# First loads on one queue, first norm and first gate projection interleaved, sums of squares by token

## The chip, the cores and the metric

The kernel runs on one core of one Trainium2 chip, in one launch. The metric is device microseconds of one execution. Three executions of the kernel before took 999.3, 1000.33 and 1001.49 us, median 1000.33. The profile comes from one further execution.

## The reference

An encoder trunk of two layers over 256 tokens of width 1024, all in float32. Each layer is FFN, mixer, FFN, and every part is a residual branch behind an RMS norm. What matters here is the first norm and the first FFN:

```python
def rms_norm(x, g):
    y = x * rsqrt(mean(x * x, axis=-1) + EPS)
    return y * g

def swiglu_ffn(h, w_gu, w_down):            # w_gu: 1024 x 5632, w_down: 2816 x 1024
    gate, up = split(h @ w_gu, 2, axis=-1)
    return (silu(gate) * up) @ w_down

x = x + 0.5 * swiglu_ffn(rms_norm(x, norm_g[0, 0]), ffn_w_gu[0, 0], ffn_w_down[0, 0])
```

Then follow a chunked gated linear attention, two more FFNs, a differential softmax attention with a relative-position bias, and a last FFN. All weights, 177 MB in all, are read once.

## The kernel before, in words

**Precision.** Each float32 operand is split in two parts that TensorE multiplies at its faster rate: a high part (ScalarE copies it, rounded) and a low part (VectorE subtracts the high part from the original). A product is three partial products. `mm3` (L207) forms them with two instructions: the weight's high part against the high and low halves of the activations (512 columns, L210), and the weight's low part against the high half (256 columns, L211). One such couple of instructions is called a pair below.

**Weights.** `weight_plan` lists all weight blocks in the order of use, mostly 1024 x 256 (1 MB). `prefetch` (L137) issues their loads on SyncE's DMA queue (SP) into three `stage` buffers; the first two blocks are loaded in four parts of 256 KB. `parts` (L152) gives the operations that split a block, one couple (high on ScalarE, low on VectorE) for each part; `split_weights` (L171) issues them up to three blocks ahead of use. `next_weights` (L194) does both and hands out the block.

**The start.** L269 loads `cst` (identity, a triangle and a column of 1/1024; 128.5 KB) on ScalarE's queue. L275 loads the norm weights as `rows`, 48 x 128, on GpSimd's queue. TensorE multiplies zeros (`ps_idle`, L280), eight products in 16 recorded instructions. `first_norm` (L446) loads x by token into `x_tm` (256, 256 and 512 columns, L452) on SP and then calls `prefetch(0)`. TensorE transposes `rows` (L455; ScalarE copies the result to `par`) and all sixteen 128 x 128 blocks of x (L462) into four PSUM tiles. Then, in an order written out with `issue_after` (which ties an instruction to one before it on the same engine), ScalarE and VectorE alternate: two column blocks of x are split with the norm's weight as scale (L321, L322), then one part of the first weights (L471). After these VectorE copies x out of PSUM (`keep`, L475), the second weights are split (L481), and x is squared block by block on ScalarE (L330, L333) and added up on VectorE (L334).

**The first FFN.** `ffn` (L490) has eleven steps c; each projects a gate block and an up block of 256 columns with `project` (L213), 16 pairs each, into two PSUM banks. Only the first gate projection runs with `together=True`: block by block of x as it becomes ready. The norm's factor by token is not needed before the products are joined: `stats` (L336) multiplies the added squares by the column of 1/1024 on TensorE (`ps_ms`, L339, four recorded instructions), and VectorE forms the reciprocal root in eleven small instructions (`rsqrt`, L253). `spread` (L344) copies it over the partitions. `join` (L246) adds the halves of a projection and so frees its banks. At c = 3 `load_params` and `relative_bias` (L773) come; the latter loads a table and 64 KB of buckets on ScalarE's queue (L776, L778).

The order of instructions on an engine is planned by the compiler: it takes the first in program order that its own model holds to be ready, and ties keep their order. So an instruction can stand ahead of another that is written before it. PSUM has six banks under tag A and two under tag B.

Of the kernel before, what the change touches and what calls it, by code (L numbers as in the profile page):

```python
# [11 lines left out]
F32 = mybir.dt.float32  # L12
FR = mybir.dt.float32r
I32 = mybir.dt.int32
AF = mybir.ActivationFunctionType
ALU = mybir.AluOpType
AX = mybir.AxisListType

P = 128
# [97 lines left out]
def trunk(ctx: ExitStack, tc: tile.TileContext, ins, out):  # L117
# [76 lines left out]
    def next_weights():  # L194
        n = state["use"]
        state["use"] += 1
        prefetch(n)
        split_weights(n)
        return split.pop(n)
# [13 lines left out]
    def project(w, act, name, together=False):  # L213
        banks = [psA.tile([P, 512], F32, tag="A", name=f"{name}_{b}") for b in range(2)]
        order = [(b, k) for b in range(2) for k in range(KD)]
        for b, k in sorted(order, key=lambda bk: bk[1]) if together else order:
            mm3(banks[b], w, slice(b * P, (b + 1) * P), act, k, k == 0, k == KD - 1)
        return banks
# [50 lines left out]
    nc.scalar.dma_start(cst, ins["c_mats"])  # L269
# [5 lines left out]
    nc.gpsimd.dma_start(rows, ins["norm_g"].rearrange("l s (k p) -> (l s k) p", p=P))  # L275
# [37 lines left out]
    class Norm:  # L313
# [22 lines left out]
        def stats(self):  # L336
            ps = psB.tile([P, 512], F32, tag="B", name=f"ps_ms{self.idx}")
            for t in range(2):
                mm(ps[:, t : t + 1], lhsT=self.acc[:, t * P : (t + 1) * P], rhs=inv_d, start=True, stop=True)  # L339
            self.var = small.tile([P, 2], F32, tag="var", name=f"var{self.idx}")  # L340
            nc.vector.tensor_scalar(out=self.var, in0=ps[:, 0:2], scalar1=EPS, scalar2=None, op0=ALU.add)
            self.r = rsqrt(self.var, [P, 2], f"r{self.idx}")
# [103 lines left out]
    def first_norm():  # L446
        n = Norm(0)
        with ExitStack() as xctx:
            xp = xctx.enter_context(tc.tile_pool(name="xin", bufs=1))
            x_tm = xp.tile([P, 2, D], F32, name="x_tm")  # L450
            for cs in (slice(0, CW), slice(CW, D // 2), slice(D // 2, D)):
                nc.sync.dma_start(x_tm[:, :, cs], ins["x"][0].rearrange("(t p) c -> p t c", p=P)[:, :, cs])  # L452
            prefetch(0)
            pst = psB.tile([P, 512], F32, tag="B", name="ps_rows")
            nc.tensor.transpose(out=pst[:, 0:NG], in_=rows, identity=ident[0:NG, 0:NG])  # L455
            nc.scalar.copy(par, pst[:, 0:NG])

            tiles = [psA.tile([P, 2, T], F32, tag="A", name=f"ps_x{i}") for i in range(KD // 2)]
            xt = [tiles[k // 4 * 2 + k % 2][:, k // 2 % 2, :] for k in range(KD)]
            for k in range(KD):  # L460
                for t in range(2):
                    nc.tensor.transpose(out=xt[k][:, t * P : (t + 1) * P], in_=x_tm[:, t, k * P : (k + 1) * P], identity=ident)  # L462
            last = ()
            for kp, ops in enumerate(parts()):
                for k in (2 * kp, 2 * kp + 1):
                    with ExitStack() as order:
                        for i in last:
                            order.enter_context(tc.issue_after(i.ins))
                        last = n.split(k, xt[k])
                with tc.issue_after(last[0].ins), tc.issue_after(last[1].ins):  # L470
                    last = [op() for op in ops]  # L471

            def keep(kp):
                k = kp // 2 * 4 + kp % 2
                return nc.vector.tensor_copy(x[:, k : k + 3 : 2, :], tiles[kp])  # L475

            with tc.issue_after(last[1].ins):
                behind = [keep(0), keep(1)]
            with tc.issue_after(behind[1].ins), tc.issue_after(last[0].ins):
                for ops in parts():  # L480
                    last = [op() for op in ops]  # L481
            with tc.issue_after(last[1].ins):
                behind = [last[0], keep(2), keep(3)]
            state["behind"] = behind
            with tc.issue_after(last[0].ins), tc.issue_after(behind[2].ins):
                for k in range(KD):
                    n.square(k)
        return n

    def ffn(norm, nxt, first=False, beside=None):  # L490
        with ExitStack() as fctx:
            fp = fctx.enter_context(tc.tile_pool(name="ffn", bufs=2))
            a2 = fp.tile([P, NFB, 2, T], FR, tag="a2", name="a2", bufs=1)
            for c in range(FF // CW):
                if first and c == 3:
                    load_params()
                    relative_bias()
# [4 lines left out]
                pg = project(next_weights(), norm.x2, f"ps_g{c}", together=first and c == 0)  # L502
                if c == 0:
                    norm.stats()
                    if not first:
                        release(*state["behind"])
# [471 lines left out]
    norm = first_norm()  # L978
    with tc.tile_pool(name="gatew", bufs=1) as gw:
        w2 = gw.tile([P, 2, GH * DK], FR, name="w2")  # L980
        norm = ffn(norm, 1, first=True, beside=lambda: load_gate(w2))
        norm = gla(norm, 2, w2)
# [47 lines left out]
```

## Time and profile before

| what | us |
|---|---|
| median of three runs | 1000.33 |
| lowest, highest | 999.3, 1001.49 |
| the profiled execution, whole | 1001.98 |
| its span, first to last instruction | 1000.2 |
| TensorE busy in the span | 990.1 |
| VectorE, ScalarE busy | 747.1, 566.4 |
| DMA: bytes read, mean rate | 176.84 MB, 179 GB/s |

The span starts with the first recorded instruction; 1.8 us of the execution lie around it. Times of a row count from the span's start. "Busy" of TensorE (PE) counts a matmul from its start to a modelled end, so that a matmul whose predecessors are slow can look longer than it is; the distance from one start to the next is the better measure. PEld is TensorE's loading of the stationary operand. DVE is VectorE, ACT ScalarE, SP the SyncE queue, and a name with q is an engine's sequencer, where DMAs are issued.

### The profile page before, as it was taken

Reading aid. Unit: us, or ns where it says so; the run is one execution under the profiler, and the core shown is the slowest. Engines: PE = TensorE matmul, PEld = TensorE weight load, DVE = VectorE, ACT = ScalarE, POOL = GpSimd, SP = SyncE. Lnnn points to the kernel's source line nnn. Section 1 sums busy time; section 2 is a strip of 40 time slices with the busy share of each in tenths; the row PEclk is TensorE's granted clock in tenths of the full one; section 3 lists DMA queues with packets and bytes.
Section 4 is the critical chain, followed back from the end, with each engine's and each line's share of the span. In section 5 each row is a group of like instructions: output and inputs, shape, how many; then the busy total and the mean of one; then the engine's idle time right before and its main releaser. Section 6 shows DMA issues by size and latency. Waiting matters only on the chain.

```text
span 1000.2 us, 14797 instructions
## 1 busy us (share of the span) xinstructions
PE 990.1 (99%) x5834; PEld 869.7 (87%) x5834; DVE 747.1 (75%) x1282; ACT 566.4 (57%) x950; POOL 2.0 (0%) x10
## 2 busy tenths in 40 slices
PE   8999999999999999999999999999999999999998
PEld 7888888998889888888888888888778998888886
DVE  6998757499977987775679777656989689767540
ACT  6766535397746755543456655435586577555430
POOL 0000000000000000000000000000000000000000
PEclk9999999999999999999999999999999999999999
DMA  9686554665322875555557655375553268555430
GB/s 291 225 262 210 183 165 131 198 223 182 102 85 86 277 227 192 177 169 178 179 175 238 206 174 186 120 238 177 203 173 127 65 193 278 182 169 198 159 126 22
DMA packets 166339, 178.87 MB, mean 179 GB/s; under 512 B 4547, under 2 KB 154846, under 8 KB 166270
## 3 DMA queue, kind: packets, MB, share of 16 engines
q1 hardware_dynamic: 165982, 177.68, 54.9%
q8 instruction: 46, 0.75, 0.3%
q10 hardware_dynamic: 256, 0.21, 0.1%
q14 instruction: 23, 0.19, 0.1%
q0 software_dynamic: 32, 0.02, 0.0%
HBM read 176.84 MB, written 1.06 MB: 178 GB/s over the span
## 4 chain that ended last, share of the span: by engine, by line
PE 69%; DVE 5%; ACT 1%; DMA 1%; issue 0%; SPq 0%; ACTq 0%
PE ps_u L210 12%; PE ps_g L210 12%; PE ps_d L210 8%; PE ps_g L211 6%; PE ps_u L211 6%; PE ps_d L211 4%; PE ps_d L225 2%; PE ps_d L227 2%; PE ps_d L226 2%; DVE w L186 1%; PE ps_s L618 1%; PE ps_w L203 1%; PE ps_w L204 1%; PE ps_w L205 1%; PE ps_g L227 1%; PE ps_g L225 1%
## 5 line engine op out<-in xcount | busy, mean ns | idle before, releaser
L186 DVE TENSOR_TENSOR w<-stage,w 128x1024 fp32r<-128x1024 f32 x332 | 384.2, 1195 | 33.2 <-ACT w L186 33.1
L186 ACT ACTIVATE w<-stage 128x1024 fp32r<-128x1024 f32 x332 | 326.9, 1035 | 55.5 <-PE ps_d L227 15.3
L210 PE MATMUL ps_g<-x,w 128*128 128x512 f32 x704 | 249.5, 397 | 0.0
L210 PE MATMUL ps_u<-x,w 128*128 128x512 f32 x704 | 248.7, 395 | 0.0
L211 PE MATMUL ps_u<-x,w 128*128 128x256 f32 x704 | 197.3, 281 | 0.0
L211 PE MATMUL ps_g<-x,w 128*128 128x256 f32 x704 | 197.1, 281 | 0.0
L210 PE MATMUL ps_d<-a,w 128*128 128x512 f32 x528 | 183.2, 390 | 0.0
L210 PEld LDWEIGHTS ps_g<-x,w 128*128 128x128 f32 x704 | 132.1, 188 | 31.1 <-issue 0.9
L210 PEld LDWEIGHTS ps_u<-x,w 128*128 128x128 f32 x704 | 132.0, 188 | 30.8
L211 PE MATMUL ps_d<-a,w 128*128 128x256 f32 x528 | 148.9, 282 | 0.0
L211 PEld LDWEIGHTS ps_g<-x,w 128*128 128x128 f32 x704 | 133.4, 189 | 0.5
L211 PEld LDWEIGHTS ps_u<-x,w 128*128 128x128 f32 x704 | 133.0, 189 | 0.1
L210 PEld LDWEIGHTS ps_d<-a,w 128*128 128x128 f32 x528 | 99.1, 188 | 20.8
L211 PEld LDWEIGHTS ps_d<-a,w 128*128 128x128 f32 x528 | 99.8, 189 | 0.0
L321 ACT ACTIVATE x<-x,par 128x256 fp32r<-128x256 f32 x40 | 20.0, 507 | 117.8 <-DVE x L370 117.8
L250 ACT COPY half<-ps_u 128x256 f32<-128x256 f32 x88 | 32.7, 372 | 86.3 <-PE ps_u L211 84.6
L250 ACT COPY half<-ps_g 128x256 f32<-128x256 f32 x88 | 32.3, 370 | 80.0 <-PE ps_g L211 78.4
L251 DVE TENSOR_TENSOR gate<-ps_g,half 128x256 f32<-128x256 f32 x88 | 36.6, 419 | 38.0 <-ACT half L250 37.9
L251 DVE TENSOR_TENSOR up<-ps_u,half 128x256 f32<-128x256 f32 x88 | 36.6, 419 | 37.8 <-ACT half L250 37.8
L370 DVE SCALAR_TENSOR_TENSOR x<-ps_d,x 128x256 f32<-128x256 f32 x48 | 20.3, 423 | 57.9 <-PE ps_d L211 56.7
L225 PE MATMUL ps_d<-w,a 128*128 128x512 f32 (+1 forms) x90 | 35.2, 391 | 0.5 <-DVE xt L441 0.5
L226 PE MATMUL ps_d<-w,a 128*128 128x512 f32 (+1 forms) x90 | 35.1, 390 | 0.0
(239 smaller groups left out, 1335.9 us busy)
## 6 DMA issues: line engine op xcount, KB each, us to landing
stage<-in_ffn_w_gu_dram SPq DMA_DIRECT2D x86, 1024.0 KB, 5.3
stage<-in_ffn_w_down_dram SPq DMA_DIRECT2D x34, 1024.0 KB, 5.3
stage<-in_gla_w_in_dram SPq DMA_DIRECT2D x12, 1024.0 KB, 5.7
stage<-in_ffn_w_down_dram SPq DMA_DIRECT2D x12, 768.0 KB, 4.5
stage<-in_diff_w_in_dram SPq DMA_DIRECT2D x16, 512.0 KB, 5.6
stage<-in_gla_w_out_dram SPq DMA_DIRECT2D x4, 1024.0 KB
stage<-in_diff_w_in_dram SPq DMA_DIRECT2D x4, 1024.0 KB
stage<-in_diff_w_out_dram SPq DMA_DIRECT2D x4, 1024.0 KB
```

What stands on the lines that cost most here:

```text
L186: op()
L203: mm(ps, lhsT=w[:, k, 0, ms], rhs=act[:, k, 0, :], start=first, stop=False)
L204: mm(ps, lhsT=w[:, k, 0, ms], rhs=act[:, k, 1, :], start=False, stop=False)
L210: mm(ps, lhsT=w[:, wk, 0, ms], rhs=act[:, k, :, :], start=first, stop=False)
L211: mm(ps[:, 0:T], lhsT=w[:, wk, 1, ms], rhs=act[:, k, 0, :], start=False, stop=last)
L225: mm(ps[:, cs], lhsT=act[:, k, 0, ts_], rhs=w[:, wk, 0, cs], start=k == 0, stop=False, **more)
L226: mm(ps[:, cs], lhsT=act[:, k, 0, ts_], rhs=w[:, wk, 1, cs], start=False, stop=False, **more)
L227: mm(ps[:, cs], lhsT=act[:, k, 1, ts_], rhs=w[:, wk, 0, cs], start=False, stop=k == nk - 1, **more)
L250: nc.scalar.copy(h[:, b, :], ps[:, T:512])
L251: nc.vector.tensor_tensor(out=out_t[:, b, :], in0=ps[:, 0:T], in1=h[:, b, :], op=ALU.add)
L321: high = nc.scalar.activation(self.x2[:, d, 0, :], src, AF.Copy, scale=g)
L370: nc.vector.scalar_tensor_tensor(out=x[:, d, :], in0=ps[:, h * T : (h + 1) * T], scalar=coef, in1=x[:, d, :], op0=ALU.mult, op1=ALU.add,)
```

## The change

The norm weights are loaded on SP, ahead of x. x comes in four loads of 256 columns, then the first weights in four parts, all on SP. Of `cst` the identity is loaded first, and the other half later, both on ScalarE's queue. The transposes of x, the splits and the first gate projection are written in one interleaved order (`first_group`), with the PSUM tiles of x dealt out differently. The squares are now taken of x by token, 1024 columns in one ScalarE instruction with an accumulated sum, two in all; `stats` takes these sums and needs no matmul. The loads of `relative_bias` are tied behind the squares. The first split of the third and fourth blocks (`split_weights(0)`) moves from the first `next_weights` to the end of `first_group`.

```diff
--- before.py
+++ after.py
@@ -210,11 +210,11 @@
         mm(ps, lhsT=w[:, wk, 0, ms], rhs=act[:, k, :, :], start=first, stop=False)
         mm(ps[:, 0:T], lhsT=w[:, wk, 1, ms], rhs=act[:, k, 0, :], start=False, stop=last)
 
-    def project(w, act, name, together=False):
+    def project(w, act, name):
         banks = [psA.tile([P, 512], F32, tag="A", name=f"{name}_{b}") for b in range(2)]
-        order = [(b, k) for b in range(2) for k in range(KD)]
-        for b, k in sorted(order, key=lambda bk: bk[1]) if together else order:
-            mm3(banks[b], w, slice(b * P, (b + 1) * P), act, k, k == 0, k == KD - 1)
+        for b in range(2):
+            for k in range(KD):
+                mm3(banks[b], w, slice(b * P, (b + 1) * P), act, k, k == 0, k == KD - 1)
         return banks
 
     def mm_tok(ps, w, act, t, k0, nk, cs=slice(None), **more):
@@ -266,13 +266,13 @@
 
     cst = const.tile([P, 2 * P + 1], F32, name="cst")
     warm = const.tile([P, 1], F32, name="warm")
-    nc.scalar.dma_start(cst, ins["c_mats"])
+    nc.scalar.dma_start(cst[:, 0:P], ins["c_mats"][:, 0:P])
     ident = cst[:, 0:P]
     tri = cst[:, P : 2 * P]
     inv_d = cst[:, 2 * P : 2 * P + 1]
     NG = 48
     rows = ev.tile([P, T], F32, tag="sq", name="rows")[0:NG, 0:P]
-    nc.gpsimd.dma_start(rows, ins["norm_g"].rearrange("l s (k p) -> (l s k) p", p=P))
+    nc.sync.dma_start(rows, ins["norm_g"].rearrange("l s (k p) -> (l s k) p", p=P))
     nc.vector.memset(warm, 0.0)
 
     idle = psB.tile([P, 512], F32, tag="B", name="ps_idle")
@@ -333,12 +333,16 @@
                 nc.scalar.activation(sq, x[:, d, :], AF.Square)
                 nc.vector.tensor_tensor(out=self.acc, in0=self.acc, in1=sq, op=ALU.add)
 
-        def stats(self):
-            ps = psB.tile([P, 512], F32, tag="B", name=f"ps_ms{self.idx}")
-            for t in range(2):
-                mm(ps[:, t : t + 1], lhsT=self.acc[:, t * P : (t + 1) * P], rhs=inv_d, start=True, stop=True)
+        def stats(self, sums=None):
+
             self.var = small.tile([P, 2], F32, tag="var", name=f"var{self.idx}")
-            nc.vector.tensor_scalar(out=self.var, in0=ps[:, 0:2], scalar1=EPS, scalar2=None, op0=ALU.add)
+            if sums is not None:
+                nc.vector.tensor_scalar(out=self.var, in0=sums, scalar1=1.0 / D, scalar2=EPS, op0=ALU.mult, op1=ALU.add)
+            else:
+                ps = psB.tile([P, 512], F32, tag="B", name=f"ps_ms{self.idx}")
+                for t in range(2):
+                    mm(ps[:, t : t + 1], lhsT=self.acc[:, t * P : (t + 1) * P], rhs=inv_d, start=True, stop=True)
+                nc.vector.tensor_scalar(out=self.var, in0=ps[:, 0:2], scalar1=EPS, scalar2=None, op0=ALU.add)
             self.r = rsqrt(self.var, [P, 2], f"r{self.idx}")
 
         def spread(self):
@@ -443,67 +447,122 @@
                         )
                         nc.sync.dma_start(out[0, ts_, ho], xt[:, t, ho])
 
-    def first_norm():
+    def first_group():
+
         n = Norm(0)
         with ExitStack() as xctx:
             xp = xctx.enter_context(tc.tile_pool(name="xin", bufs=1))
             x_tm = xp.tile([P, 2, D], F32, name="x_tm")
-            for cs in (slice(0, CW), slice(CW, D // 2), slice(D // 2, D)):
+            src, nk, width, _ = plan[0]
+            t0 = staged[0] = stage.tile([P, nk, width], F32, tag="stage", name="stage0")
+            state["dma"] = 1
+
+            def load_x(kp):
+                cs = slice(kp * CW, (kp + 1) * CW)
                 nc.sync.dma_start(x_tm[:, :, cs], ins["x"][0].rearrange("(t p) c -> p t c", p=P)[:, :, cs])
+
+            def load_w(kp):
+                ks = slice(2 * kp, 2 * kp + 2)
+                nc.sync.dma_start(t0[:, ks, :], src.rearrange("(k p) n -> p k n", p=P)[:, ks])
+
+            for load in (load_x, load_w):
+                for kp in range(KD // 2):
+                    load(kp)
+            nc.scalar.dma_start(cst[:, P:], ins["c_mats"][:, P:])
             prefetch(0)
             pst = psB.tile([P, 512], F32, tag="B", name="ps_rows")
             nc.tensor.transpose(out=pst[:, 0:NG], in_=rows, identity=ident[0:NG, 0:NG])
             nc.scalar.copy(par, pst[:, 0:NG])
 
             tiles = [psA.tile([P, 2, T], F32, tag="A", name=f"ps_x{i}") for i in range(KD // 2)]
-            xt = [tiles[k // 4 * 2 + k % 2][:, k // 2 % 2, :] for k in range(KD)]
-            for k in range(KD):
-                for t in range(2):
-                    nc.tensor.transpose(out=xt[k][:, t * P : (t + 1) * P], in_=x_tm[:, t, k * P : (k + 1) * P], identity=ident)
+            xt = [tiles[k % 4][:, k // 4, :] for k in range(KD)]
+            ops = list(parts())
+            banks = [psA.tile([P, 512], F32, tag="A", name=f"ps_g0_{b}") for b in range(2)]
+            w0 = split.pop(0)
+            state["use"] = 1
             last = ()
-            for kp, ops in enumerate(parts()):
+
+            def turn(kp):
                 for k in (2 * kp, 2 * kp + 1):
-                    with ExitStack() as order:
-                        for i in last:
-                            order.enter_context(tc.issue_after(i.ins))
-                        last = n.split(k, xt[k])
-                with tc.issue_after(last[0].ins), tc.issue_after(last[1].ins):
-                    last = [op() for op in ops]
+                    for t in range(2):
+                        nc.tensor.transpose(out=xt[k][:, t * P : (t + 1) * P], in_=x_tm[:, t, k * P : (k + 1) * P], identity=ident)
+
+            def in_order(call):
+                nonlocal last
+                with ExitStack() as order:
+                    for i in last:
+                        order.enter_context(tc.issue_after(i.ins))
+                    last = call()
+
+            def split_x(kp):
+                for k in (2 * kp, 2 * kp + 1):
+                    in_order(lambda: n.split(k, xt[k]))
+
+            def split_w(kp):
+                in_order(lambda: [op() for op in ops[kp]])
+
+            def multiply(kp):
+                for k in (2 * kp, 2 * kp + 1):
+                    for b in range(2):
+                        mm3(banks[b], w0, slice(b * P, (b + 1) * P), n.x2, k, k == 0, k == KD - 1)
+
+            turn(0)
+            turn(1)
+            split_x(0)
+            split_x(1)
+            split_w(0)
+            turn(2)
+            multiply(0)
+            split_x(2)
+            split_w(1)
+            turn(3)
+            multiply(1)
+            split_x(3)
+            split_w(2)
+            multiply(2)
+            split_w(3)
+            multiply(3)
 
             def keep(kp):
-                k = kp // 2 * 4 + kp % 2
-                return nc.vector.tensor_copy(x[:, k : k + 3 : 2, :], tiles[kp])
+                return nc.vector.tensor_copy(x[:, kp : kp + 5 : 4, :], tiles[kp])
 
             with tc.issue_after(last[1].ins):
                 behind = [keep(0), keep(1)]
             with tc.issue_after(behind[1].ins), tc.issue_after(last[0].ins):
-                for ops in parts():
-                    last = [op() for op in ops]
+                for both in parts():
+                    last = [op() for op in both]
+            sums = small.tile([P, 2], F32, tag="sums", name="sums", bufs=1)
+            with tc.issue_after(last[0].ins):
+                for t in range(2):
+                    sq = xp.tile([P, D], F32, tag="xsq", name="xsq")
+                    squared = nc.scalar.activation(sq, x_tm[:, t, :], AF.Square, accum_out=sums[:, t : t + 1])
             with tc.issue_after(last[1].ins):
-                behind = [last[0], keep(2), keep(3)]
+                behind = [squared, keep(2), keep(3)]
             state["behind"] = behind
-            with tc.issue_after(last[0].ins), tc.issue_after(behind[2].ins):
-                for k in range(KD):
-                    n.square(k)
-        return n
-
-    def ffn(norm, nxt, first=False, beside=None):
+            split_weights(0)
+        return n, banks, sums
+
+    def ffn(norm, nxt, first=None, beside=None):
         with ExitStack() as fctx:
             fp = fctx.enter_context(tc.tile_pool(name="ffn", bufs=2))
             a2 = fp.tile([P, NFB, 2, T], FR, tag="a2", name="a2", bufs=1)
             for c in range(FF // CW):
                 if first and c == 3:
                     load_params()
-                    relative_bias()
+                    with tc.issue_after(state["behind"][0].ins):
+                        relative_bias()
                 if beside is not None and c == 6:
                     beside()
                 if c == 0 and not first:
                     state["hold"] = "low"
-                pg = project(next_weights(), norm.x2, f"ps_g{c}", together=first and c == 0)
-                if c == 0:
+                if first and c == 0:
+                    pg, sums = first
+                    norm.stats(sums)
+                else:
+                    pg = project(next_weights(), norm.x2, f"ps_g{c}")
+                if c == 0 and not first:
                     norm.stats()
-                    if not first:
-                        release(*state["behind"])
+                    release(*state["behind"])
                 gate = fp.tile([P, 2, T], F32, tag="gate", name="gate")
                 join(pg, gate)
                 pu = project(next_weights(), norm.x2, f"ps_u{c}")
@@ -975,10 +1034,10 @@
             out_proj(o2, n2, [range(0, 3), range(3, 6), range(6, 8)], [lambda: flip(3), lambda: attend(3), lambda: release(*normalize(3))])
         return n2
 
-    norm = first_norm()
+    norm, *gate0 = first_group()
     with tc.tile_pool(name="gatew", bufs=1) as gw:
         w2 = gw.tile([P, 2, GH * DK], FR, name="w2")
-        norm = ffn(norm, 1, first=True, beside=lambda: load_gate(w2))
+        norm = ffn(norm, 1, first=gate0, beside=lambda: load_gate(w2))
         norm = gla(norm, 2, w2)
     norm = ffn(norm, 3)
     norm = ffn(norm, 4)
```

## Rows read from the trace of the kernel before

**Rows 1.** Head of the page: the span, and busy time of the engines.

```profile
span 1000.2 us, 14797 instructions
PE 990.1 (99%) x5834; PEld 869.7 (87%) x5834; DVE 747.1 (75%) x1282; ACT 566.4 (57%) x950; POOL 2.0 (0%) x10
```

**Rows 2.** Waits of TensorE, 15.5 to 600 us, whole answer (total, times, longest).

```profile
PE ps_s L618 <- DVE qkd L658: 0.2, 1, 0.2
```

**Rows 3.** The same from 600 us to the end: the longest of five lines.

```profile
PE ps_doT L947 <- DVE do L939: 1.7, 2, 1.0
```

**Rows 4.** Timeline of TensorE, start (start, duration, instruction, count, wait before it).

```profile
0.92 3.42 PE L280 MATMUL ps_idle<-warm 128*128 128x128 f32 x16 [0.92 <-DVE warm L276]
5.40 0.26 PE L455 MATMUL ps_rows<-cst,rows 48*128 48x48 f32 x1 [1.06 <-DMA rows<-in_norm_g_dram]
5.59 1.09 PE L462 MATMUL ps_x<-cst,x_tm 128*128 128x128 f32 x8
7.48 1.97 PE L462 MATMUL ps_x<-cst,x_tm 128*128 128x128 f32 x8 [0.80 <-DMA x_tm<-in_x_dram]
9.09 1.20 PE L210 MATMUL ps_g<-x,w 128*128 128x512 f32 x2
...
10.52 0.46 PE L210 MATMUL ps_g<-x,w 128*128 128x512 f32 x1
...
15.49 0.62 PE L210 MATMUL ps_u<-x,w 128*128 128x512 f32 x2
```

**Rows 5.** Timeline of ScalarE, start.

```profile
6.56 0.84 ACT L321 ACTIVATE x<-ps_x,par 128x256 fp32r<-128x256 f32 x2 [0.67 <-PE ps_x L462]
8.18 0.63 ACT L471 ACTIVATE w<-stage 128x512 fp32r<-128x512 f32 x1 [0.78 <-DMA stage<-in_ffn_w_gu_dram]
```

**Rows 6.** Timeline of VectorE, start.

```profile
8.85 0.69 DVE L471 TENSOR_TENSOR w<-stage,w 128x512 fp32r<-128x512 f32 x1 [0.90 <-ACT w L471]
...
13.01 0.68 DVE L471 TENSOR_TENSOR w<-stage,w 128x512 fp32r<-128x512 f32 x1
...
25.50 0.42 DVE L251 TENSOR_TENSOR gate<-ps_g,half 128x256 f32<-128x256 f32 x1
```

**Rows 7.** Windows (PE, PEld, DVE, ACT, POOL busy; granted clock, DMA share, GB/s).

```profile
2.00:2.50 0.50, 0.50 (x4) 0.50 (x4) 0.00 (x0) 0.21 (x1) 0.00 (x0) 1.00 0.73 125
...
7.00:7.50 0.50, 0.02 (x1) 0.03 (x1) 0.43 (x2) 0.40 (x2) 0.00 (x0) 0.73 1.10 363
...
10.00:11.00 1.00, 1.00 (x6) 0.86 (x5) 1.00 (x3) 1.00 (x4) 0.00 (x0) 0.68 1.10 347
```

**Rows 8.** DMA issues, first 5 us (KB each, median us to landing).

```profile
x_tm<-in_x_dram SPq DMA_DIRECT2D x2, 256.0 KB, 3.6
...
cst<-in_c_mats_dram ACTq DMA_DIRECT2D x1, 128.5 KB
oh<-in_c_buckets_dram ACTq DMA_DIRECT2D x1, 64.0 KB
rows<-in_norm_g_dram POOLq DMA_DIRECT2D x1, 24.0 KB, 4.1
```

**Rows 9.** Timeline of SP, start: the three issues of x.

```profile
0.74 1.46 SPq L452 DMA_DIRECT2D x_tm<-in_x_dram  x3
```

**Rows 10.** Timeline of TensorE around the norm's matmuls.

```profile
26.77 0.40 PE L210 MATMUL ps_u<-x,w 128*128 128x512 f32 x1
27.01 0.50 PE L339 MATMUL ps_ms<-cst,acc 128*128 128x1 f32 x4
...
27.57 0.39 PE L210 MATMUL ps_u<-x,w 128*128 128x512 f32 x1
```

**Rows 11.** Groups of instructions, 6 to 31 us (count, busy and mean ns, idle before).

```profile
L334 DVE TENSOR_TENSOR acc<-acc,sq 128x256 f32<-128x256 f32 x7 | 2.9, 417 | 0.6 <-ACT sq L333 0.5
L333 ACT ACTIVATE sq<-x 128x256 f32<-128x256 f32 x7 | 2.8, 410 | 0.0
...
L260 DVE SCALAR_TENSOR_TENSOR r_t<-r_y 128x2 f32<-128x2 f32 x3 | 0.5, 158 | 0.1
```

## The prediction

> **What bounds the kernel now.** I read the busy times first: TensorE is busy for 990.1 of 1000.2 us, VectorE for 747.1, ScalarE for 566.4 [rows 1]. A busy TensorE need not be a fed one, so the waits come next. From 15.5 to 600 us TensorE waits for 0.2 us in all [rows 2]; behind 600 us, in the differential attention, a few waits add up, the longest group 1.7 us [rows 3]. So from 15.5 us on the kernel is a row of matmuls. Only three things move its end: a matmul taken out of the row, the moment at which the row begins, and the waits late in the attention. VectorE and ScalarE work that is saved counts only where TensorE waits for it.
>
> The row begins like this [rows 4]. Zeros are multiplied until 4.34 us. TensorE then waits 1.06 us for the norm weights, transposes the first half of x, waits 0.80 us for the second half, transposes it (7.48 to 9.45), and starts the first gate projection at 9.09. The second projection starts at 15.49. That start is my mark: what it moves by, the end moves by.
>
> Between 9.09 and 10.52 two pairs were done, 0.71 us each; the other 14 of the 16 pairs took 4.97 us, 0.355 each [rows 4]. The windows say why: the granted clock is 0.73 on average in 7.0 to 7.5 and 0.68 in 10 to 11 [rows 7], so TensorE ran at the lower of its two levels, 1.2 GHz, from about 7.23 (0.54 of that half microsecond at half speed) to 10.64 (0.64 of that microsecond), after the two waits. The fast pairs ran without a gap: in the projection itself nothing is left but its start and the clock.
>
> **The change part by part.** *The norm's matmuls go.* The four ps_ms instructions (L339) stand in the row: the matmul ahead of them starts at 26.77, the next couple's at 27.57 [rows 10], 0.80 us where a pair takes 0.355. The change saves 0.45 us. No cover is needed, since TensorE is the bound there; below 0.45 it goes only if something else then ends last at that place.
>
> *Loads.* Norm weights waited for at 5.40 came by GpSimd's queue, 4.1 us from issue to landing; a quarter of x by SP took 3.6 [rows 8]. Put first on SP they land with the identity, no later than x. Three issues on SP took 1.46 us [rows 9], so every later load on SP is issued 0.49 us later than now. Ahead of the first part of the weights, which landed at 8.18 [rows 5], stand 64 KB fewer (the 64 KB of buckets goes behind the squares) or 128 KB fewer (if the second half of cst is issued late as well) [rows 8]. At 363 GB/s [rows 7] this is 0.18 to 0.36 us. The 0.49 shows only as far as the engines run dry at the start; at 2.0 to 2.5 us they moved 125 GB/s [rows 7], so there is room to hide it, and to lose it. Bounds for the first weights: 8.18 - 0.36 = 7.82 and 8.18 + 0.49 - 0.18 = 8.49. I take 8.0, nearer the early end, because norm weights and identity fill the time that x gives up.
>
> The norm weights' 24 KB and the full x stand ahead of the weights in both kernels. The Trainium skill, DMA: Bandwidth & Descriptors, section "Issuing engines are not separate DMA queues", says that loads issued by SP, ScalarE and GpSimd run on the same engines and that several issuers save issue time alone; this speaks against the move. By it the 0.49 shows in full, the weights come at about 8.4, and the sum below would be 0.45 instead of 0.65 us.
>
> *Transposes and x's splits.* The first x split had to wait 0.67 us for TensorE and ran at 6.56 [rows 5]. With x landing at 0.74 + 3.6 = 4.3 to 4.8, and a further quarter each 0.72 us (256 KB at 363 GB/s), transposes of a quarter take 0.55 us (eight in 1.09 [rows 4]), at the lower clock 1.0 (eight in 1.97). All of x can be turned by 8.3, and half of it split on ScalarE and VectorE, before the weights can be used. The same 16 transposes stay; they only move into time in which TensorE waits.
>
> *Start of the products.* ScalarE splits the first part in 0.63 us [rows 5]: 8.0 + 0.63 + 0.07 = 8.7, against 9.09 now. If the clock runs as now, 1.2 GHz until about 10.5, the 0.39 us buy 0.39/0.71 = 0.55 pairs, which are worth 0.55 x 0.355 = 0.20 us once the clock is up. With the bounds of the weights, 0.4 us to either side of 8.0 or so, this term is 0 to 0.3 us.
>
> *Lower parts.* VectorE's four weight parts start 1.39 us apart, 8.85 to 13.01 [rows 6], a couple of x blocks between each. In the new order the third and fourth follow each other: first at 8.67, last at 8.67 + 2 x 1.39 + 0.69 = 12.1, done at 12.8. TensorE wants it for the 13th pair, at 10.52 + (12 - 2.55) x 0.355 = 13.9. Hidden by 1.1 us; at 2.4 GHz throughout it wants it at 8.7 + 12 x 0.355 = 13.0, and the second part's low half (done at 10.75) at 10.1, which I count as 0.3 us of waiting in that case.
>
> *Squares and root.* Seven additions of 0.417 us leave VectorE [rows 11]. Eight squares of 0.41 us leave ScalarE; the two new ones, over 1024 columns with a sum, are not in the trace of before. Between one old square and four each they cost 0.8 to 3.3 us together, at most what goes. The eleven small root instructions, 0.16 us each [rows 11], only come earlier, ahead of the join. That could bite: the join's last addition ends at 25.92 [rows 6] and the projection that takes its banks starts at 26.77, 0.85 us later [rows 10]. VectorE loses 2.9 us, gains 1.8 to 2.2 ahead of the join and is about 0.9 us earlier at the end of the first splits; so the margin stays over 0.85 + 0.9 - 1.25 = 0.5 us even if TensorE gains the most. I cost this part at nothing.
>
> **Sum.** 0.45 + 0.20 = 0.65 us. The profiled execution took 1001.98 us, 1.8 beyond its span, and would take 1001.3. The median of the runs is 1.65 lower than that execution; the same gain from 1000.33 gives 999.7.
>
> **The rivals.** *A, forecast:* as above, 999.7, chance 0.45; its own range, with the bounds of the weights and the runs' own scatter, is 998.9 to 1000.6.
>
> *B, the clock stays up.* Without the two waits TensorE may keep 2.4 GHz. Then the projection ends at 8.7 + 16 x 0.355 + 0.3 = 14.7 instead of 15.49: 0.8 + 0.45 = 1.25 us, 999.1. For it: the waits of 1.06 and 0.80 us in front of the drop get shorter. Against it: transposes are spread out more thinly, and TensorE still stands idle before 8.7. Chance 0.2.
>
> *C, slower: the slow stretch slides under the products.* The stretch at 1.2 GHz lasted 3.4 us, of which 1.55 lay under products. If the clock is still high at 8.7 and drops behind that, all 3.4 us lie under products and cost 1.7 us: 8.7 + 5.7 + 1.7 + 0 to 0.3 = 16.1 to 16.4, 0.6 to 0.9 later than now; less 0.45 this is 0.15 to 0.45 slower, 1000.6. It decides from the moment at which the drop comes after 8.7 instead of before. The idle time between the last transposes and 8.7 speaks for it, the many transposes right before it against it. The Trainium skill, TensorE: Matmul & The Clock Gate, Part 1, holds that the low clock is the default and activity lifts it; the drop after the two waits agrees, and B and C are the two ways in which that may come out. Chance 0.15.
>
> *D, the change does not do what it says.* The last four transposes are written behind the first products. If they stay there, 0.55 to 1.0 us comes into the row, and 0.65 turns into -0.35 to 0.1: about 1000.4. The planner takes what is ready, and the last quarter of x is ready before the weights; chance 0.08.
>
> *E, a replanned attention.* The order of all later instructions is planned anew from shifted times. A lost or doubled longest wait there [rows 3] moves the end by 1.7 us either way: 998.0 or 1001.4. Nothing in the profile speaks for one side; chance 0.12.
>
> **How the numbers follow.** Fewer than 0.2%, 2.0 us, can't be told from no change here: the three runs are 2.2 us apart. A, B, C and D lie within that bound; E's good half reaches past it, and scatter takes some of B with it. Faster by over 0.2%: 0.18. Slower by over it, E's bad half and an unseen stall in the join: 0.12. Same: 0.70. The range takes in E's two ends with a little scatter, 997.7 to 1001.6.
>
> **What would show it.** The ps_ms couple of c = 0 missing from TensorE's row; ps_rows at about 4.4 instead of 5.40; the first weight part landing at 7.8 to 8.5; ps_u starting at about 15.3 (A), 14.7 (B), 16.1 to 16.4 (C). Transposes between gate products would show D. The prediction is wrong if TensorE waits between 15 and 60 us, for weights or a bank, or if its waits behind 600 us change by more than 1 us.

## The result, and the profile after

The changed kernel takes 1006.72 us (median of 6 runs, 1004.9 to 1007.58) where the kernel before takes 1000.38 (6 runs, 999.3 to 1001.58): ratio 1.0051, interval 1.0035 to 1.0066. It is slower, and outside the range of the prediction.

The head of the page after (columns as in [rows 1]) has the first hint:

```profile
span 1005.1 us, 14771 instructions
PE 995.3 (99%) x5830; PEld 870.4 (87%) x5830; DVE 745.3 (74%) x1275; ACT 566.1 (56%) x946; POOL 1.4 (0%) x9
```

The span grew by 4.9 us and TensorE's busy time by 5.2, with four matmuls fewer. So TensorE hardly waits more; the same matmuls take longer. It is not the clock: from 15.5 us on the granted clock is 1.00 in both. The waits agree: these are all of TensorE's from 15.5 to 600 us, and the longest one behind 600 us, against [rows 2] and [rows 3].

```profile
PE ps_s L677 <- DVE qkd L717: 0.4, 1, 0.4
...
PE ps_doT L1006 <- DVE do L998: 1.7, 2, 1.0
```

Which matmuls, the groups by form tell (count, busy us, mean ns of one, idle before). First the main matmul of the down projections (the downs, below) in the kernel before, then the same line after:

```profile
L210 PE MATMUL ps_d<-a,w 128*128 128x512 f32 x528 | 183.2, 390 | 0.0
```

```profile
L210 PE MATMUL ps_d<-a,w 128*128 128x512 f32 x528 | 186.7, 396 | 0.0
```

Same count, same shape, no idle time, 3.5 us more. These matmuls come from 136 us on, far from anything that the diff touches. The starts in the trace show it sharper: a pair (128x512, then 128x256; 768 columns) begins either 346.7 or 353.3 ns after the one ahead, as a mean over six pairs, for hundreds of pairs on end. At 2.4 GHz that is 832 or 848 cycles. I call them fast and slow pairs. Of some 1,830 pairs classed this way, 1154 were fast before and 509 after: 645 x 6.6 ns = 4.3 us of the 4.9.

The front, TensorE's timeline (columns as in [rows 4], which it answers):

```profile
4.63 0.34 PE L474 MATMUL ps_rows<-cst,rows 48*128 48x48 f32 x1
4.90 1.63 PE L488 MATMUL ps_x<-cst,x_tm 128*128 128x128 f32 x8
7.20 0.63 PE L488 MATMUL ps_x<-cst,x_tm 128*128 128x128 f32 x4 [0.67 <-DVE x L322]
...
9.40 1.20 PE L210 MATMUL ps_g<-x,w 128*128 128x512 f32 x2 [0.92 <-ACT w L502]
10.39 0.63 PE L488 MATMUL ps_x<-cst,x_tm 128*128 128x128 f32 x2
...
16.90 0.40 PE L210 MATMUL ps_u<-x,w 128*128 128x512 f32 x1
```

and ScalarE's first weight part, against [rows 5]:

```profile
8.72 0.63 ACT L502 ACTIVATE w<-stage 128x512 fp32r<-128x512 f32 x1 [1.46 <-DMA stage<-in_ffn_w_gu_dram]
```

The second projection starts 1.41 us later than before. The windows (columns as in [rows 7]; the granted clock is the third number from the end) show TensorE at 1.2 GHz under the products:

```profile
9.00:9.50 0.50, 0.10 (x1) 0.10 (x1) 0.12 (x1) 0.50 (x2) 0.00 (x0) 0.96 1.07 375
...
11.00:12.50 1.50, 1.50 (x7) 1.31 (x6) 1.50 (x4) 1.44 (x4) 0.00 (x0) 0.50 1.10 348
12.50:13.00 0.50, 0.50 (x4) 0.43 (x3) 0.50 (x2) 0.50 (x3) 0.00 (x0) 0.63 1.11 352
```

Once ps_ms ([rows 10]) and the root's broadcast (ps_r, from `spread`) have passed in both, the difference between the traces falls from 1.40 to 0.95 us. Then it grows evenly, 0.08 us in 12 pairs or 6.7 ns a pair, from 47 to 195, 446 to 505 and 630 to 688 us; from 892 to 930 us it shrinks at the same rate, and it stands between these stretches, but for small steps in the two attentions.

### The profile page after: what moved, and what is told of

Read it like the earlier page. It is cut to its first block, busy times and chain, and to the rows that moved or that the text cites. A ratio compares the mean times of both kernels' runs of the same rounds, so it can differ in the third digit from the quotient of the medians.

```text
span 1005.1 us, 14771 instructions
## 1 busy us (share of the span) xinstructions
PE 995.3 (99%) x5830; PEld 870.4 (87%) x5830; DVE 745.3 (74%) x1275; ACT 566.1 (56%) x946; POOL 1.4 (0%) x9
## 3 DMA queue, kind: packets, MB, share of 16 engines
HBM read 176.84 MB, written 1.06 MB: 177 GB/s over the span
## 4 chain that ended last, share of the span: by engine, by line
PE 68%; DVE 5%; ACT 2%; issue 1%; ACTq 0%
PE ps_u L210 12%; PE ps_g L210 12%; PE ps_d L210 8%; PE ps_g L211 6%; PE ps_u L211 6%; PE ps_d L211 4%; PE ps_d L225 2%; PE ps_d L227 2%; PE ps_d L226 2%; DVE w L186 2%; PE ps_s L677 1%; PE ps_w L203 1%; PE ps_w L204 1%; PE ps_w L205 1%; ACT w L186 1%; PE ps_g L225 1%
## 5 line engine op out<-in xcount | busy, mean ns | idle before, releaser
L210 PE MATMUL ps_d<-a,w 128*128 128x512 f32 x528 | 186.7, 396 | 0.0
```

The costliest lines, as they stand in the source:

```text
L210: mm(ps, lhsT=w[:, wk, 0, ms], rhs=act[:, k, :, :], start=first, stop=False)
```

## The experiments

Theories at the start: the front (loads and interleaving) or the squares by token with their new order set the later pace; or the pace comes from neither. All ratios are against the kernel before, run on the same chip beside it.

**Both kernels again**, unchanged.

> The kernel before once more, unchanged, for a second profile. Pace theory: a pair of projection matmuls takes 346.7 or 353.3 ns, the pace is kept until an instruction of another shape stands in TensorE's row, and it is set by the program: the second profile shows the same stretches at the same pace (fast from 46 to 193, 443 to 508 and 517 to 687 us; slow from 331 to 443 and from 820 us on), about 1150 fast and 670 slow pairs, 1000 us. Rival, chance: the pace is drawn anew in each execution, and the stretches differ between the two profiles.

> The changed kernel once more, unchanged, for a second profile. Pace theory: about 510 fast and 1330 slow pairs again, slow from 47 to 197 and from 335 to 510 us, 1005 to 1007 us. Rival, chance: other stretches are slow, and the time moves by up to 4 us.

One run each: 998.6 and 1005.56 us. The pace differs from execution to execution (1507 fast pairs in the kernel before this time, 427 after), but the downs stayed fast before and slow after. In neither was there a low clock at the front, and the front differed less. TensorE's first product, before and then after:

```profile
8.57 0.73 PE L210 MATMUL ps_g<-x,w 128*128 128x512 f32 x2 [0.31 <-ACT w L471]
```

```profile
9.10 0.73 PE L210 MATMUL ps_g<-x,w 128*128 128x512 f32 x2 [0.88 <-ACT w L502]
```

**Each half of the change alone.** sums_only is the kernel before with the squares by token; front_only is the changed kernel with the old squares and ps_ms.

```diff
 # sums_only, against before
+            sums = small.tile([P, 2], F32, tag="sums", name="sums", bufs=1)
...
+                    squared = nc.scalar.activation(sq, x_tm[:, t, :], AF.Square, accum_out=sums[:, t : t + 1])
...
-                    n.square(k)
 # front_only, against after
-            sums = small.tile([P, 2], F32, tag="sums", name="sums", bufs=1)
...
+                    n.square(k)
```

> The kernel before with one part of the change: the first norm's sums of squares by token on ScalarE, no norm matmuls; loads, transposes and the first projection as before. In TensorE's row two norm matmuls go and the two that spread the factor move ahead by some 20 pairs; nothing else differs. Pace theory: the first projection ends at 15.5 us as before, 0.45 us go with the matmuls, but from the place of the two spread matmuls on the pace is set anew: a stretch that flips costs or gives 6.6 ns a pair (425 pairs between 46 and 193 us: 2.8 us), so the time is anywhere from 997 to 1005 and the profile's count of slow pairs accounts for it within 0.5 us. Rival, front alone: no stretch changes its pace and the time is 999.9.

> The changed kernel with one part undone: squares by block and norm matmuls as before; loads on one queue and the interleaved first projection stay. Rival, front alone: the second projection starts at 16.9 us as in the changed kernel, 1.4 us later than before, the norm matmuls' 0.45 us come back, and the paces are those of the kernel before: 1001.8. Pace theory: the same 1.4 us, and besides them 6.6 ns for each pair that is slow here and fast in the kernel before; anywhere from 999 to 1008, accounted for by the count of slow pairs within 0.5 us.

sums_only: 1005.81 us, 1.0051 [1.0033, 1.0070]. front_only: 1001.38, 1.0011 [0.9995, 1.0026], although this profile had the low clock under the products as well (ps_u at 17.15). So the squares carry the loss, and the front does not. In sums_only this is TensorE's only wait from 15.5 to 600 us, so no wait explains the loss:

```profile
PE ps_s L623 <- DVE qkd L663: 0.2, 1, 0.2
```

What else the squares bring is a tile: eight bytes in the pool of small tiles, padded to 32, which moves every tile allocated behind that pool. Among them is a2, the split hidden activations that the downs stream through TensorE. x2, the split input that the gate and up projections stream, lies ahead of that pool and stays.

**The tile's bytes without its instructions.** An unused 32 bytes is added; the instructions and their order on each engine are those of the kernel before (or of after, for after_...). For "on64" I moved things by 32 bytes more, to see whether multiples of 64 mend it.

```diff
 # before_act_off32 and after_act_on64: everything behind the small tiles
-            nlam = small.tile([P, 1], F32, tag="nlam", name="nlam", bufs=1)
+            nlam = small.tile([P, 9], F32, tag="nlam", name="nlam", bufs=1)[:, 0:1]
 # after_all_on64 (this alone) and before_all_on64 (both): everything behind cst
-    cst = const.tile([P, 2 * P + 1], F32, name="cst")
+    cst = const.tile([P, 2 * P + 9], F32, name="cst")[:, 0 : 2 * P + 1]
```

> The kernel before with 32 bytes more for one small tile (nlam is 9 floats wide instead of 1, only the first is used). No instruction changes; all tiles allocated behind the small pool move by 32 bytes, as the new tile of sums moves them in the changed kernel. So the hidden activations a2, which the down projections stream, start 32 bytes off a multiple of 64, where they started on one. Layout theory: in the three down projections that stream a2 (174 pairs each, fast in all three profiles of the old layout) a pair takes 353.3 instead of 346.7 ns: 522 x 6.6 ns = 3.5 us slower, about 1004.4. Rival, order: the pace is set by where the norm's and the spread's matmuls stand in TensorE's row; the row is that of before, so the time stays at 1000.9 and the down projections stay fast.

> The changed kernel with the same 32 bytes more, which bring a2 back on a multiple of 64; no instruction changes. Layout theory: the three down projections are fast again, 3.5 us off, about 1002.7 instead of 1006.2; the gate and up projections, whose x2 starts 32 bytes off in both kernels, may run at either pace. Rival, order: the time and the paces stay, 1005.5 to 1006.7.

> The changed kernel with the constant tile cst 32 bytes wider: stage, weights w, x2 and a2 all start on multiples of 64. Layout theory: no slow pair is left; the profiles of the changed kernel had 1332 and 1414 slow pairs, 6.6 ns each, 8.8 to 9.3 us: about 997. Rival, order: 1005.5 to 1006.7 with slow stretches as before.

> The kernel before with both paddings: stage, w, x2 and a2 all on multiples of 64. Layout theory: the 314 to 671 slow pairs of the two profiles go, 2.1 to 4.4 us, about 997.5, and the scatter from run to run shrinks. Rival, order or chance: 1000.9 as before, with slow stretches in the gate and up projections.

before_act_off32: 1005.63 us, 1.0038 [1.0023, 1.0053]. Its downs are those of the changed kernel:

```profile
L210 PE MATMUL ps_d<-a,w 128*128 128x512 f32 x528 | 186.7, 396 | 0.0
```

Not one instruction changed, and the loss is there, 1.2 us more than I expected: gate and up of the first two feed-forwards were slow as well. But "multiples of 64" is false: after_act_on64 1003.81, 1.0023 [1.0013, 1.0034]; after_all_on64 1004.98, 1.0037 [1.0024, 1.0050]; before_all_on64 1004.56, 1.0027 [1.0011, 1.0043].

**The instructions without the tile's bytes.** The sums go into the padding of an existing tile, so no address moves. sums_same_layout is the same edit on sums_only.

```diff
-    warm = const.tile([P, 1], F32, name="warm")
+    spare = const.tile([P, 8], F32, name="warm")
+    warm = spare[:, 0:1]
...
-            sums = small.tile([P, 2], F32, tag="sums", name="sums", bufs=1)
+            sums = spare[:, 2:4]
```

> The changed kernel with the two sums of squares kept in the free end of a tile that was padded anyway, so that no tile's address differs from the kernel before; the order of instructions on each engine is that of the changed kernel. Address theory: the products' pairs go back to the pattern of the kernel before, down projections at 346.7 ns a pair, over 1100 fast pairs in all; only the front's loss (some +1.4 us at the second projection, less 0.45 for ps_ms) is left, so 1000.5 to 1002.0 us, ratio 1.000 to 1.002. Rival (the order or the phase of the changed instructions sets the pace): as the changed kernel, 1005 to 1007 us, about 500 fast pairs.

> The kernel before with the sums by token alone, and these two sums in the free end of a padded tile, so that no address moves. Address theory: 999.5 to 1001 us, over 1100 fast pairs, a ratio of 0.998 to 1.001 (0.45 us gained from ps_ms). Rival (squares by token change the pace): 1005.8, as the same kernel took with a tile of its own for the sums.

after_same_layout: 1001.63 us, 0.9998 [0.9982, 1.0014], its downs at 390 ns again:

```profile
L210 PE MATMUL ps_d<-a,w 128*128 128x512 f32 x528 | 183.2, 390 | 0.0
```

sums_same_layout: 1001.78, 1.0000 [0.9986, 1.0014]; its median is 0.8 us above what I expected, its profile has 1001 fast pairs in place of over 1100. This settles the cause: the 32 bytes alone bring the loss, and without them no loss is left that these intervals (0.0014 to 0.0016 to either side) would show.

**Which address, and what period.** before_gate_off32 moves only gate, sg and up, tiles that VectorE and ScalarE work on; the others move everything behind the small tiles by 256 or 128 bytes.

```diff
 # before_gate_off32
-            a2 = fp.tile([P, NFB, 2, T], FR, tag="a2", name="a2", bufs=1)
+            a2 = fp.tile([P, NFB * 2 * T + 8], FR, tag="a2", name="a2", bufs=1)[:, 0 : 0 + NFB * 2 * T].rearrange("p (k h t) -> p k h t", k=NFB, h=2)
 # before_act_off256: nlam 65 floats wide; before_act_off128: 33
```

> The kernel before with the feed-forward tile a2 allocated 32 bytes longer, the first part used: a2, x2 and the weights stay where they were, only gate, sg and up of the feed-forwards (what VectorE and ScalarE work on) move by 32 bytes. If it is the address of what TensorE streams (a2) that counts, the down projections stay fast (346.7 ns a pair) and the time is 1000 to 1001.5 us; if it is where the other engines read and write, the downs are slow and the time is 1004.5 to 1006.

> The kernel before with every tile behind the small ones moved by 256 bytes instead of 32. If the pace goes by addresses modulo 256 bytes (or a divisor of it), the pattern is that of the kernel before: downs fast, 1000 to 1001.5 us. If any move away from the old addresses costs, or the period is longer, the downs are slow and the time is 1003.5 to 1006.

> The kernel before with everything behind the small tiles moved by 128 bytes. Period of 128 bytes: downs fast, 1000 to 1001.5 us. Period of 256: downs slow in the first three feed-forwards as with 32 and 64 bytes, 1003.5 to 1006 us.

before_gate_off32: downs at 390 ns, 1002.82 us, 1.0015 [1.0004, 1.0026]; a2's address counts, not that of VectorE's tiles, though the time lies between my two forecasts (919 fast pairs). before_act_off256: downs fast, 1000.51, 0.9995 [0.9985, 1.0006]. before_act_off128: downs at 346.7 ns too, so the period is 128 bytes and not 256; it took 1002.77, 1.0013 [1.0000, 1.0027], 1.3 us over what I expected. Its profiled execution (1002.74) had a front that ran 2.0 us later than in the kernel before (ps_u at 17.45); of the others no front is on record.

**Own address, or distance to the weights.** By the sizes of the tiles in the kernel before, a2 lies 32 bytes beyond a multiple of 128 from the weight tiles, x2 at a multiple. The first two kernels give x2 the 32 bytes; the third moves the weights under a2; the last two put x2 at 64 and 96. In all five a2's own address moves by 256.

```diff
 # before_x2_off32 and after_x2_off32 (+ 8); before_x2_off64: + 16; before_x2_off96: + 24
-    x = xpool.tile([P, KD, T], F32, tag="x", name="x")
+    x = xpool.tile([P, KD * T + 8], F32, tag="x", name="x")[:, 0 : KD * T].rearrange("p (k t) -> p k t", k=KD)
 # before_w_off32: cst 2 * P + 9 floats wide
 # in each: nlam widened so that a2 ends 256 bytes behind its old address
```

> The kernel before with x2 (what the gate, up and attention projections stream) moved by 32 bytes and everything behind the small tiles by 256, so that x2 stands to the weights as a2 does in the kernel before (32 bytes beyond a multiple of 256; before, x2 stood at a multiple). Distance theory: gate and up projections take the pace that the downs had, 346.7 ns a pair in nearly all stretches, over 1600 fast pairs, 996.5 to 999 us, ratio 0.995 to 0.998. Rival (x2's pace does not go by that distance): as before, a mixture of both paces in gate and up, 1000 to 1002 us. Rival (any 32-byte step of x2 costs): all gate and up pairs slow, 1002 to 1005.

> The changed kernel with its own tile for the sums, x2 moved by 32 bytes, and everything behind the small tiles by 256 in all against the kernel before (the sums' tile included). Distance theory: as in the kernel before with x2 moved, less 0.45 us for ps_ms, plus 0 to 1.4 at the front: 996.5 to 999.5 us. Rival (order of the changed instructions counts, or x2's distance does not): 1000 to 1002.

> The kernel before with weights and x2 moved by 32 bytes and a2 by 256: a2's own address modulo 256 is that of before, its distance to the weights is 0 instead of 32, x2 stands to the weights as before. Distance theory: the downs no longer run fast throughout (they take either pace, as x2 did at distance 0), x2's stretches as before: 1001 to 1004 us. Rival (a2's own address counts): the downs are fast, 1000 to 1001.5.

> The kernel before with x2 moved by 64 bytes, a2 by 256 (so a2 keeps its distance of 32 bytes to the weights). Distance theory: all gate and up pairs of the four feed-forwards slow (353.3 ns), the downs fast, some 600 to 750 fast pairs of 1825: (1154 - 650) x 6.6 ns = 3.3 us more than the profiled kernel before, 1003 to 1005.5 us. Rival (x2's pace does not follow a2's rule): a mixture as before or fast, 997 to 1001.5.

> The kernel before with x2 moved by 96 bytes, a2 by 256. Distance theory: as with 64 bytes, gate and up slow, downs fast, 1003 to 1005.5 us. Rival (only one of the two distances is slow, or none): 997 to 1001.5.

before_x2_off32: 997.48 us, 0.9956 [0.9942, 0.9969], 1820 fast pairs, 5 slow. after_x2_off32: 997.44, 0.9955 [0.9939, 0.9971], 1838 fast, 3 slow. **Both beat both kernels.** The three groups of before_x2_off32:

```profile
L210 PE MATMUL ps_g<-x,w 128*128 128x512 f32 x704 | 247.2, 392 | 0.0
L210 PE MATMUL ps_u<-x,w 128*128 128x512 f32 x704 | 246.3, 390 | 0.0
...
L210 PE MATMUL ps_d<-a,w 128*128 128x512 f32 x528 | 183.2, 390 | 0.0
```

before_x2_off64: 1006.04, 1.0056 [1.0039, 1.0073], half a microsecond beyond what I expected. Gate and up are slow throughout, with the downs as before:

```profile
L210 PE MATMUL ps_g<-x,w 128*128 128x512 f32 x704 | 251.2, 397 | 0.0
L210 PE MATMUL ps_u<-x,w 128*128 128x512 f32 x704 | 250.6, 396 | 0.0
...
L210 PE MATMUL ps_d<-a,w 128*128 128x512 f32 x528 | 183.2, 390 | 0.0
```

before_x2_off96: 1002.57, 1.0015 [1.0006, 1.0025], less than expected, because 96 bytes give a third pace, 350.0 ns a pair, halfway:

```profile
L210 PE MATMUL ps_g<-x,w 128*128 128x512 f32 x704 | 248.8, 394 | 0.0
L210 PE MATMUL ps_u<-x,w 128*128 128x512 f32 x704 | 248.7, 394 | 0.0
```

before_w_off32, with a2 and x2 both at a multiple: 997.96, 0.9964 [0.9952, 0.9975], faster than I expected. The downs took over the pace ahead of them: slow in the first feed-forward, fast in the other two.

The feed-forwards of all 20 profiles fit one table, of the distance of the streamed tile from the weights modulo 128 bytes:

| distance | pair | cycles at 2.4 GHz | seen with |
|---|---|---|---|
| 32 | 346.7 ns | 832 | a2 before, also with 128 or 256 added; x2 in x2_off32 |
| 64 | 353.3 ns | 848 | a2 in the changed kernel, off32, all_on64; x2 in x2_off64 |
| 96 | 350.0 ns | 840 | a2 in after_act_on64; x2 in x2_off96 |
| 0 | 346.7 or 353.3 | 832 or 848 | x2 in all others; a2 in w_off32 |

a2 at 96, in after_act_on64, gives the downs this row, between the two paces above:

```profile
L210 PE MATMUL ps_d<-a,w 128*128 128x512 f32 x528 | 185.0, 393 | 0.0
```

At distance 0 the pace is not all chance: the third feed-forward's gate and up came out fast in all 16 profiles that have x2 there.

It is the distance and not the own address: x2 lies at the same address in before_x2_off32 (all fast) and in before_all_on64 (weights moved along; gate and up slow in the first two feed-forwards).

## Why the prediction was wrong

*The step that failed* is the sum's silent one: "Only three things move its end: a matmul taken out of the row, the moment at which the row begins, and the waits late in the attention." A fourth does, the pace of the row. I read 0.355 us a pair from the front and took it for a constant. The edit to blame stands under "Squares and root ... I cost this part at nothing": its instructions cost almost nothing, its eight bytes of memory 5 us. a2's distance goes from 32 to 64; 528 down pairs x 6.6 ns are 3.5 us, just what the ps_d row shows. The rest fits the gate and up pairs of the first two feed-forwards, at distance 0, though that is a count over few profiles and not a test. With a2 at 64 or 96 bytes they were slow in 7 of 7 profiles each; with a2 at 32 and x2 at 0, slow in 4 of 8 and 5 of 8. Of 254 and 317 pairs, half and three eighths more are 246 x 6.6 ns = 1.6 us. The sum, 5.1 us, is close to what lies between the changed kernel (1.0051) and after_same_layout (0.9998): 0.0053, or 5.3 us. Whether a2's place tips these pairs, and why it should, is open.

My own test for being wrong missed it: TensorE did not wait between 15 and 60 us and its waits behind 600 did not move by 1 us, so rival E, a replanned attention, did not come either.

*Norm's matmuls*, -0.45: the traces agree (1.40 to 0.95, as told above). But part is given back. The root's broadcast now stands earlier in the row (ps_r at 28.44 instead of 30.63), and in 4 of 8 profiles with sums by token TensorE waits for it, 0.9 to 1.8 us. In after_x2_off32 these rows show it, TensorE's wait first, then VectorE and ScalarE:

```profile
PE ps_r L351 <- DVE r_y L262: 0.9, 1, 0.9
```

```profile
24.45 0.16 DVE L260 SCALAR_TENSOR_TENSOR r_t<-r_y 128x2 f32<-128x2 f32 x1
25.96 0.42 DVE L251 TENSOR_TENSOR gate<-ps_g,half 128x256 f32<-128x256 f32 x1 [1.35 <-ACT half L250]
26.30 0.15 DVE L261 TENSOR_TENSOR r_t<-r_t,var 128x2 f32<-128x2 f32 x1
```

```profile
23.66 2.01 ACT L186 ACTIVATE w<-stage 128x1024 fp32r<-128x1024 f32 x2 [1.90 <-DMA stage<-in_ffn_w_gu_dram]
25.57 0.35 ACT L250 COPY half<-ps_g 128x256 f32<-128x256 f32 x1
```

The root's last steps stand behind a join on VectorE, which waits for a copy on ScalarE, which stands behind weight splits that waited 1.90 us for their load. I had looked for "that could bite" at the join's banks; it bit one step further. The two new squares took 1.06 + 0.19 us each, 2.5 together, inside my 0.8 to 3.3.

*Loads.* I took 8.0 for the first weights, with bounds 7.82 to 8.49; 8.72 is outside. Here a term was mis-sized: two more issues stand ahead of the weights on SP, the norm weights and a fourth quarter of x, and I counted one. So SP issues the first weights 0.93 us later and not 0.49; with 0.93 the late bound would have been 8.93, and 8.72 inside. The kernel before, then the changed one:

```profile
2.24 2.81 SPq L148 DMA_DIRECT2D stage<-in_ffn_w_gu_dram  x4
```

```profile
0.73 0.39 SPq L275 DMA_DIRECT2D rows<-in_norm_g_dram  x1
1.18 1.95 SPq L462 DMA_DIRECT2D x_tm<-in_x_dram  x4
3.17 2.01 SPq L466 DMA_DIRECT2D stage<-in_ffn_w_gu_dram  x4
```

ScalarE starts the first weight part at 8.26 to 8.94 in the seven profiles with the new front (median 8.44) and at 7.68 to 9.13 in the thirteen with the old (median 8.18). The Trainium skill, DMA: Bandwidth & Descriptors, section "Issuing engines are not separate DMA queues", holds that several issuers save issue time alone, which spoke against the move; the medians lean its way, by 0.26 us, but within a scatter of 1.5. *Clock.* Rival C came in the profiled execution: the whole stretch at 1.2 GHz lay under products, and ps_u started at 16.90 where C said 16.1 to 16.4, since the products began at 9.40 and not at 8.7. It is not the rule: a stretch at 1.2 GHz came in 2 of 7 profiles with the new front and 3 of 13 with the old. *D* was half right: two of the last transposes stand behind the first products. Over all profiles ps_u starts at 15.11 (median; 14.89 to 17.15) with the new front and 15.27 (14.36 to 17.45) with the old, so the 0.20 us that I took for the start is far smaller than the difference from one execution to the next.

At equal pace the change is worth nothing that can be measured: after_x2_off32 and before_x2_off32 differ by 0.04 us in the median, with intervals of 0.0013 to 0.0016 to either side. Those intervals are wider than the forecast's gain of 0.65 us, so whether it is in there can't be told.

*What stays open.* Weights, their staging tiles and x moved together in every kernel, so the distance could be to any of the three; the weights are what TensorE reads beside the stream. Why a distance costs 8 or 16 cycles a pair was not tested. Open too is what tips the pace at distance 0.

## What to carry to other kernels

A kernel that is one row of matmuls has a pace, and the pace can depend on where tiles lie: before costing an edit at nothing, count the bytes that it allocates and which tiles move. When busy time grows with fewer instructions and no waits, compare the mean duration of one shape between the kernels, and then test with padding alone. A new scratch tile is best put into padding that is there; and the distance between streamed tile and weights is a parameter worth trying, here 32 bytes modulo 128, which gave 0.45% for two lines.

## What the runs showed of the hardware

Three paces of the same pair, 832, 840 and 848 cycles, by 32-byte steps of the distance, and two at distance 0, of which one holds for hundreds of pairs. The Trainium skill, SBUF — State Buffer, section "Who interferes with whom", gives TensorE two independent read ports, one for the stream and one for the weight load, and says that "PE and ACT never wait on anyone". No wait is seen here either, but the pace changes by 2% with the distance of the streamed tile from the weights (or from what moves with them); the measurement decides. The two paces at distance 0 can also explain much of how far runs of the kernel before lie apart (997.5 to 1004 us): in its two profiles 46 to 134, 331 to 443 and 820 to 932 us came out fast in one and slow in the other, some 870 pairs or 5.8 us at stake. The five runs each of before_x2_off32 and after_x2_off32 lie within 2.1 and 2.6 us.
